# A two-layer decoder kernel: the second head's sums of weights are made in the second unit in place of the fourth

## The chip, the core and the metric

The kernel runs on one core of one Trainium2 chip. The metric is the device time of one execution, in microseconds. The core has a matrix engine (TensorE, PE in the profile; its weight loads are shown apart as PEld), a vector engine (DVE), a scalar engine (ACT), a general engine (GpSimd, POOL) and a sync engine (SP), which here issues nearly all DMAs. Each engine takes its instructions in an order fixed when the kernel is built, and waits where an instruction's inputs or buffers aren't ready.

## What is computed

The input is a sequence of 2048 rows of 1024 numbers. A retention layer comes first, then a layer of attention within a sliding window. The change touches the first layer only:

```python
proj = rmsnorm(x, g_norm) @ w_in                # 1024 -> q 1024, k 1024, v 2048, gate 2048
q, k = theta_shift(q), theta_shift(k)           # 4 heads of 256
v                                               # 4 heads of 512
o = rms(retention(q, k, v))                     # chunks of 128 rows, a state of 256 x 512 per head
x = x + (o * silu(gate)) @ w_out
```

The second layer computes one shared K and V, 16 query heads over 128 keys back with a bias and a sink, a gate and an output product. All is float32; the kernel splits operands into a high and a low part, so that one product becomes three matmuls.

## The kernel before, in words

The first layer is done in 16 **units**: four groups of 512 rows, and in each the four heads. Unit u is group u // 4, head u % 4, and units are counted from 0, so the second unit is unit 1 and the fourth is unit 3. For each unit `main` (L500) makes the products with the weights: q and k in `project_qk` (L564), then the values and the gate; `ret` (L655) does the retention of the unit in four chunks of 128 rows; `out_a` (L779) multiplies with the output weights and adds to the rows. The loop at the end of `phase_a` runs `main` of unit u + 1 together with `ret` of unit u (through `drive`, L43, which takes turns between the two) and then `out_a` of unit u.

Values and gate are made in two ways. Units 0 to 3 (`plain_vg`, L615) multiply as usual. From unit 4 on, `strassen` (L445) makes a value block and a gate block with seven products in place of eight. It needs sums and differences of weights, and of rows:

- `stage_sums(h)` (L376) makes the **sums of weights** of head h, once, and writes them to DRAM. It takes eight pieces; each piece is two loads of 256 KB (L393), four DVE operations of 128x256 (L397 to L400) and, one step later, two stores of 256 KB (L387). Head h's sums are first read in unit 4 + h.
- `row_stats(g)` (L300) loads the rows of group g (L307) and takes the mean of their squares on ACT (L309).
- `stage_rows(g)` (L317), the **row staging**, turns the result with PE (`spread`, L170), scales the rows of group g (L343), makes their sums (L347 to L350) and writes both to DRAM (L331). `load_sums` (L371) and `load_rows` (L366) read them back through `load_part` (L362, with an ACT cast at L363 and a DVE subtraction at L364). For group 1 this is called in unit 3.

These three are generators. They stand in a list, `behind`, and `step()` (L290) advances the first of the list by one; it is taken off when it has ended. `step()` is called at fixed places of the code: four times in `project_qk`, four times each in the value and the gate product of units 0 to 3, fourteen times in `strassen`, and six times in `out_a`. So units 1, 2 and 3 have 18 steps each and the units from 4 on 24. `stage_sums` takes 11 steps, `row_stats` 5 and `stage_rows` 12. Before, `behind` gets head 0 at unit 1, the row statistics and row staging of group 1 at unit 2, head 1 at unit 3, head 2 at unit 4 and head 3 at unit 5.

The places of the steps set the order of the code, which isn't the order of execution by itself: when the kernel is built, a scheduler runs through the code with a model of the times and puts an instruction on its engine as soon as its inputs are there and a buffer is free, code that comes first having the preference. Buffers come from pools by tag. All of the work in `behind`, and the split rows that `out_a` makes at the end of a group (L786), use the tag "st" with six buffers. Weights and rows that come from DRAM go through the tag "raw" with three (L118 to L126, L307, L362).

The other lines that are spoken of are in `ret`: the square of an output block (ACT, L748), the mean and power on POOL (L114, L115), the gated block (DVE, L751), its transpose (PE, L754), the state (DVE, L739 and L741), its high and low part (ACT L828, DVE L829), the products with it (PE, L726 to L728) and with the chunk (L718 to L720, L729 to L731); and in `out_a` the evacuation that adds a PSUM bank to the rows (DVE, L794). PSUM banks "a" and "b" (two each) serve all products with weights in turn, so a product can start only when the evacuations of the one before are done.

Of the kernel before, what the change touches and what calls it, by code (L numbers as in the profile page):

```python
# [42 lines left out]
def drive(tc, main, side, ratio, ahead, head=0):  # L43

    main_on = side_on = True
    due = head - ratio
    while main_on or side_on:
        due += ratio
        while main_on and (due >= 1 or not side_on):
            main_on = next(main, "end") != "end"  # L50
            due -= 1
        if side_on:
            with tc.high_priority(offset=ahead):
                side_on = next(side, "end") != "end"
# [3 lines left out]
def tile_yoco(ctx, tc, x, x_t, w_qk, w_vg, wo_a, w_kv, w_b, wo_b, ag, kvg, bg, kng, qng,  # L58
# [116 lines left out]
    def scales(g, tiles, tag, rb):  # L175

        acc, rt = tiles
        nc.sync.dma_start(acc, sqs[g])
        yield
        ps = bank(f"ssq_{g}", tag)  # L180
        for m in range(MT):
            nc.tensor.matmul(ps[:, m : m + 1], acc[:, m * P : (m + 1) * P], ones[:, :1], start=True, stop=True)
        r, eps = (small.tile([P, MT], F32, tag=f"{n}bx", bufs=2, name=f"{n}bx_{g}") for n in ("r", "e"))
        nc.vector.tensor_scalar(eps, ps[:, :MT], 1.0 / D, EPS, op0=ALU.mult, op1=ALU.add)
        nc.gpsimd.tensor_tensor(r, eps, neghalf[:, :MT], op=ALU.pow)
        nc.vector.tensor_scalar_mul(eps, eps, EPS)
        scaled[g] = r, eps, rb
        yield
        load = spread(r, rt, f"b{g}", tag)
        yield  # L190
        yield
        load(rb)
        yield
# [84 lines left out]
    def phase_a(pa):  # L278
# [9 lines left out]
        behind = []  # L288

        def step():  # L290
            if behind and next(behind[0], "end") == "end":
                behind.pop(0)
# [4 lines left out]
        def short(name):  # L297
            return p1.tile([P, 512], F32, tag="r", bufs=4, name=name)

        def row_stats(g):  # L300

            ss = small.tile([P, MT], F32, tag="ssx", bufs=2, name=f"ssx_{g}")
            r = small.tile([P, MT], F32, tag="rx", bufs=2, name=f"rx_{g}")
            st["stats", g] = ss, r
            for m in range(MT):
                xin = wp.tile([P, D], F32, tag="raw", bufs=RAW, name=f"xin_{g}_{m}")
                nc.sync.dma_start(xin, x[(g * MT + m) * P : (g * MT + m + 1) * P, :])  # L307
                junk = p1.tile([P, D], BF16, tag="st", bufs=6, name=f"jx_{g}_{m}")
                nc.scalar.activation(junk, xin, AF.Square, accum_out=ss[:, m : m + 1])  # L309
                if m == MT - 1:  # L310
                    nc.gpsimd.tensor_scalar(ss, ss, 1.0 / D, EPS, op0=ALU.mult, op1=ALU.add)
                    nc.gpsimd.tensor_tensor(r, ss, neghalf[:, :MT], op=ALU.pow)
                yield
# [62 lines left out]
        def stage_sums(h):  # L376

            vg = w_vg[h]

            d = [dram.tile([2, 2, P, 2, 512], F32, name=f"T{i}v_{h}") for i in range(2)]  # L380
            st["sums", h] = {"T2": d[0][0], "T1": d[0][1], "T4": d[1][0], "T3": d[1][1]}
            pieces = [(c, slice(256 * e, 256 * e + 256)) for c in range(4) for e in range(2)]
            raw, done = [], []
            for n in range(len(pieces) + 2):

                for c, e, i, t in done:
                    nc.sync.dma_start(d[i][:, c // 2, :, c % 2, e].rearrange("j p t -> p j t"), t)  # L387
                done = []
                if n < len(pieces):
                    c, e = pieces[n]  # L390
                    raw.append([p1.tile([P, 2, 256], F32, tag="st", bufs=6, name=f"b{h}_{n}_{i}") for i in range(2)])
                    for i in range(2):
                        nc.sync.dma_start(raw[n][i], vg[i, :, c // 2, :, c % 2, e].rearrange("j p t -> p j t"))  # L393
                if 0 < n <= len(pieces):
                    c, e = pieces[n - 1]
                    (b11, b12), (b21, b22) = [[t[:, j, :] for j in range(2)] for t in raw[n - 1]]
                    nc.vector.tensor_tensor(b22, b22, b12, op=ALU.subtract)  # L397
                    nc.vector.tensor_tensor(b12, b12, b11, op=ALU.subtract)
                    nc.vector.tensor_tensor(b11, b22, b11, op=ALU.add)
                    nc.vector.tensor_tensor(b21, b21, b11, op=ALU.subtract)  # L400
                    done = [(c, e, i, raw[n - 1][i]) for i in range(2)]
                yield

        def stage_b(pieces):

            raw, done = [], []
            for n in range(len(pieces) + 2):
                if n < len(pieces):
                    t = p1.tile(list(pieces[n][0].shape), F32R, tag="st", bufs=6, name=f"wlo_{n}")
                    nc.sync.dma_start(t.bitcast(F32), pieces[n][0])  # L410
                    raw.append(t)
                for d, i, v in done:
                    nc.sync.dma_start(d[:, i], v.bitcast(F32))
                done = []
                if 0 < n <= len(pieces):
                    t = raw[n - 1]
                    _, d, sc = pieces[n - 1]
                    hi = p1.tile(list(t.shape), F32R, tag="st", bufs=6, name=f"whi_{n}")
                    for k in range(t.shape[1]):
                        v, h = t[:, k, :], hi[:, k, :]  # L420
                        if sc is None:
                            nc.scalar.copy(h, v.bitcast(F32))
                            nc.vector.tensor_tensor(v, v.bitcast(F32), h.bitcast(F32), op=ALU.subtract)
                        else:
                            nc.scalar.mul(h, v.bitcast(F32), sc[:, k : k + 1])
                            nc.vector.scalar_tensor_tensor(v, v.bitcast(F32), sc[:, k : k + 1], h.bitcast(F32),
                                                           op0=ALU.mult, op1=ALU.subtract)
                    done = [(d, 0, hi), (d, 1, t)]
                yield
# [405 lines left out]
        for u in range(nu - 1):  # L835

            g, h = units[u + 1]
            if u + 1 in (1, 3, 4, 5):
                behind.append(stage_sums({1: 0, 3: 1, 4: 2, 5: 3}[u + 1]))
            if h == 2 and g + 1 < NG:  # L840
                behind.append(row_stats(g + 1))
                behind.append(stage_rows(g + 1))
            if u + 1 in (8, 9, 12, 13, 14, 15):
                behind.append(stage_b(todo[:9]))
                del todo[:9]
            if u + 1 == nu - 1:
                behind.append(scales(0, [short(f"stb_{i}") for i in range(2)], "rr", small.tile([P, T], F32, tag="rb", bufs=1, name="rb_0")))
            drive(tc, main(u + 1), ret(u), 2 if u + 1 < PLAIN else 3, 0)
            for _ in itertools.islice(bias, 2 if u >= RH else 0):
                pass  # L850
            if u < nu - 2:
                for _ in out_a(u):
                    step()
# [383 lines left out]
    with ExitStack() as es:  # L1237
        mk = lambda name, bufs: es.enter_context(tc.tile_pool(name=name, bufs=bufs))
        psum["phase"] = "a"
        psum["pool"] = es.enter_context(tc.tile_pool(name="psa", bufs=1, space=bass.MemoryType.PSUM))  # L1240
        phase_a(dict(v=mk("av", 4), const=mk("ca", 1), p1=mk("a1", 1), p2=mk("a2", 2), g=mk("ag", 4), xs=mk("as", 1), x1=mk("ax", MT)))
# [97 lines left out]
```

## Time and profile before

| what | value |
|---|---|
| median of 3 runs | 2459.9 us (2458.28 to 2459.98) |
| the profiled execution | 2457.89 us |
| its span, first to last instruction | 2456.2 us |
| PE busy | 2410.0 us, 98% |
| PE weight loads busy | 1963.2 us, 80% |
| DVE busy | 1592.5 us, 65% |
| ACT busy | 1056.4 us, 43% |
| POOL busy | 281.8 us, 11% |
| moved by DMA | 501.76 MB, 204 GB/s on average |

Times in the profile are microseconds from the span's start. A group's row names the line, the engine, the operation and the tiles (out<-in). In a row of instructions in order of time, the first number is the start and the second the duration, and a bracket gives how long the engine was idle before it and what ended that. In a row of waits the numbers are the sum of the waits in us, how many there were, and the longest. A row of a window gives its ends, its length and each engine's busy time with the number of instructions in parentheses. PE's matmuls overlap, so that busy time is the union of their spans. "granted clock" is the share of full speed that TensorE was given.

### The profile page before, as it was taken

The page shows a single profiled execution, that of the slowest core. Times are in us where ns is not written, and L with a number is a line of the kernel's source. Part 1 is how long each engine was busy: PE and PEld are TensorE (multiplying, and loading weights), DVE is VectorE, ACT ScalarE, POOL GpSimd, SP SyncE. Part 2 cuts the span into 40 slices and gives each one's busy share as a digit, 9 for nine tenths or more (in the row PEclk, how much of TensorE's full clock was granted, in tenths as well). Part 3 has the DMA queues.
Part 4 walks back from the last instruction along what each step waited for, and adds up shares of the span by engine and source line. Part 5 has one row for each costly group of instructions (what it writes and reads, how often), then busy time and mean ns, then how long its engine had stood idle before and what let it go on. Part 6 is the DMA issues. An engine that isn't in the chain of part 4 may idle for free.

```text
span 2456.2 us, 32234 instructions
## 1 busy us (share of the span) xinstructions
PE 2410.0 (98%) x11569; PEld 1963.2 (80%) x11569; DVE 1592.5 (65%) x2874; ACT 1056.4 (43%) x2028; POOL 281.8 (11%) x348
## 2 busy tenths in 40 slices
PE   8999999999999999999999999999999999999997
PEld 6888778888878888888888788887787787778776
DVE  5646684787768668587777864744656556466555
ACT  4333233544446356355445643533424334334332
POOL 0000000021000020000002000122202212202020
PEclk9999999999999999999999999999999999999999
DMA  8433884488676368386548953646564674665662
GB/s 286 152 112 116 280 285 129 155 300 279 210 263 216 129 238 283 129 289 224 173 155 296 342 185 103 206 147 227 202 206 146 223 258 137 206 202 185 201 230 69
DMA packets 195379, 501.76 MB, mean 204 GB/s; under 512 B 20487, under 2 KB 65748, under 8 KB 195220
## 3 DMA queue, kind: packets, MB, share of 16 engines
q1 hardware_dynamic: 195140, 499.45, 60.6%
q8 instruction: 91, 1.49, 0.2%
q14 instruction: 68, 0.56, 0.1%
q0 software_dynamic: 80, 0.26, 0.0%
HBM read 397.88 MB, written 104.90 MB: 205 GB/s over the span
## 4 chain that ended last, share of the span: by engine, by line
PE 83%; DMA 9%; DVE 4%; ACT 2%; issue 1%; SPq 1%; POOL 0%; ACTq 0%; DVEq 0%; POOLq 0%
PE pp_ao L146 4%; PE pp_ao L148 4%; PE pp_ao L147 4%; PE o_t L1153 3%; PE s_t L1104 2%; PE pp_bo L267 2%; PE pp_bo L268 2%; PE pp_bo L266 2%; PE pT_t L1135 1%; DMA xS<-xss 1%; DMA b<-in_w_vg 1%; PE dl_r L718 1%; PE dl_r L720 1%; PE ot_r L754 1%; PE dl_r L719 1%
## 5 line engine op out<-in xcount | busy, mean ns | idle before, releaser
L1107 DVE CUSTOM_DVE_ANT_0 P_t<-s_t,bias,nsnk 128x256 f32<-128x256 f32 (+1 forms) x256 | 116.5, 472 | 132.2 <-PE s_t L1104 124.4
L146 PE MATMUL pp_ao<-ohi_r,whi_ao 128*128 128x512 f32 x512 | 199.6, 391 | 0.9 <-DVE x_r L794 0.9
L147 PE MATMUL pp_ao<-olo_r,whi_ao 128*128 128x512 f32 x512 | 199.6, 390 | 0.0
L148 PE MATMUL pp_ao<-ohi_r,wlo_ao 128*128 128x512 f32 x512 | 193.7, 390 | 0.0
L1117 ACT ACTIVATE P_t<-P_t,nm_t 128x128 f32<-128x128 f32 x256 | 100.5, 395 | 113.9 <-DVE P_t L1114 111.5
L114 POOL TENSOR_SCALAR r_o_r<-sso_r,ep 128x1 f32<-128x1 f32 x48 | 36.8, 766 | 908.1 <-ACT jo_r L748 908.1
L794 DVE TENSOR_TENSOR x_r<-x_r,pp_ao 128x512 f32<-128x512 f32 x128 | 86.3, 683 | 62.1 <-PE pp_ao L148 62.0
L828 ACT CAST Shi_r<-S 128x512 fp32r<-128x512 f32 x120 | 69.8, 618 | 121.2 <-PE o_r L728 80.7
L146 PEld LDWEIGHTS pp_ao<-ohi_r,whi_ao 128*128 128x128 f32 x512 | 96.1, 188 | 21.8 <-ACT whi_a3qk L125 1.1
L148 PEld LDWEIGHTS pp_ao<-ohi_r,wlo_ao 128*128 128x128 f32 x512 | 96.1, 188 | 20.3 <-DVE wlo_ao L126 0.2
L147 PEld LDWEIGHTS pp_ao<-olo_r,whi_ao 128*128 128x128 f32 x512 | 96.1, 188 | 19.8
L1104 PEld LDWEIGHTS s_t<-kst,qst_b 128*128 128x128 f32 x512 | 83.1, 193 | 31.5 <-DVE nm_t L1107 7.5
L125 ACT CAST whi_ao<-raw_ao 128x1024 fp32r<-128x1024 f32 x64 | 67.1, 1050 | 91.2 <-DMA raw_ao<-in_wo_a 33.7
L829 DVE TENSOR_TENSOR Slo_r<-S,Shi_r 128x512 fp32r<-128x512 f32 x120 | 79.0, 686 | 37.0 <-ACT Shi_r L828 36.7
L1104 PE MATMUL s_t<-kst,qst_b 128*128 128x256 f32 (+1 forms) x512 | 98.3, 295 | 4.6 <-DVE nm_t L1107 4.6
L126 DVE TENSOR_TENSOR wlo_ao<-raw_ao,whi_ao 128x1024 fp32r<-128x1024 f32 x64 | 78.2, 1223 | 36.9 <-ACT whi_ao L125 36.7
L1141 POOL TENSOR_SCALAR_AFFINE_SELECT pTs_t<-pTs_t 128x512 f32<-128x512 f32 x60 | 40.4, 674 | 524.5 <-ACT pTs_t L1138 524.5
L741 DVE SCALAR_TENSOR_TENSOR S<-S,dl_r 128x512 f32<-128x512 f32 x112 | 74.2, 682 | 33.8 <-PE dl_r L720 33.8
L1138 ACT COPY pTs_t<-pT_t 128x512 f32<-128x512 f32 x64 | 37.4, 584 | 132.3 <-PE pT_t L1135 132.0
L267 PE MATMUL pp_bo<-olo_t,whi_bo 128*128 128x512 f32 x224 | 88.1, 393 | 0.4 <-DVE olo_t L1174 0.3
L268 PE MATMUL pp_bo<-ohi_t,wlo_bo 128*128 128x512 f32 x224 | 87.9, 393 | 0.0
L266 PE MATMUL pp_bo<-ohi_t,whi_bo 128*128 128x512 f32 x224 | 85.6, 397 | 1.2 <-ACT ohi_t L1172 1.1
(1036 smaller groups left out, 7137.8 us busy)
## 6 DMA issues: line engine op xcount, KB each, us to landing
raw_ao<-in_wo_a SPq DMA_DIRECT2D x64, 512.0 KB, 3.7
b<-in_w_vg SPq DMA_DIRECT2D x64, 256.0 KB, 5.2
res<-xmid SPq DMA_DIRECT2D x28, 512.0 KB, 6.0
whi_bo<-wo SPq DMA_DIRECT2D x28, 512.0 KB, 3.9
wlo_bo<-wo SPq DMA_DIRECT2D x28, 512.0 KB, 4.7
x_r<-in_x_t SPq DMA_DIRECT2D x16, 512.0 KB, 6.9
xin<-in_x SPq DMA_DIRECT2D x16, 512.0 KB, 3.4
T0v<-b SPq DMA_DIRECT2D x32, 256.0 KB, 5.3
```

The lines of the kernel that those rows point to most:

```text
L126: nc.vector.tensor_tensor(lo, raw, hi.bitcast(F32), op=ALU.subtract)
L146: nc.tensor.matmul(o, hi[:, kk, sl], xh, start=st, stop=False)
L147: nc.tensor.matmul(o, hi[:, kk, sl], xl, start=False, stop=False)
L148: nc.tensor.matmul(o, lo[:, kk, sl], xh, start=False, stop=sp)
L266: nc.tensor.matmul(o, hi[:, kk, sl], xh, start=s, stop=False)
L267: nc.tensor.matmul(o, hi[:, kk, sl], xl, start=False, stop=False)
L268: nc.tensor.matmul(o, lo[:, kk, sl], xh, start=False, stop=e)
L794: nc.vector.tensor_tensor(t, t, ps, op=ALU.add)
L829: nc.vector.tensor_tensor(lo, src[:, d, :], hi.bitcast(F32), op=ALU.subtract)
L1104: nc.tensor.matmul(o, q[:, h, :], kst[:, kv * 2 + hl, kb + b0 : kb + 2, :], start=hl == 0, stop=hl == 1)
L1107: nc.vector.tensor_tensor_reduce(out=pt[:, j, :w], in0=o, in1=bias[:, kv * GQ + h, b0 * P :], scale=-1.0, scalar=nsnk[:, kv * GQ + h : kv ...
L1117: nc.scalar.activation(pt[:, i, :P], pt[:, i, :P], AF.Exp, scale=-1.0, bias=nm[:, i : i + 1], accum_out=den[:, i : i + 1])
```

## The change

The list `behind` gets heads 0 and 1 together at unit 1, and nothing of heads at unit 3. Heads 2 and 3 are put in where they were, and nothing else is changed. Head 1's eleven steps then stand behind head 0's: of the 18 steps in unit 1 head 0 takes 11 and head 1 seven, its last four come in unit 2, and the row statistics and the row staging of group 1, 17 steps, follow behind these; three of the 17 fall into unit 3.

```diff
         for u in range(nu - 1):
 
             g, h = units[u + 1]
-            if u + 1 in (1, 3, 4, 5):
-                behind.append(stage_sums({1: 0, 3: 1, 4: 2, 5: 3}[u + 1]))
+            for head in {1: (0, 1), 4: (2,), 5: (3,)}.get(u + 1, ()):
+                behind.append(stage_sums(head))
             if h == 2 and g + 1 < NG:
                 behind.append(row_stats(g + 1))
                 behind.append(stage_rows(g + 1))
```

## The prediction

> **What bounds the kernel now.** I read the page's head and its chain first, then PE's busy time unit by unit, then PE's waits in the unit that stands out, then the streams of single engines there. Units are counted from 0: the second unit is unit 1, the fourth is unit 3.
>
> ```profile
> span 2456.2 us, 32234 instructions
> PE 2410.0 (98%) x11569; PEld 1963.2 (80%) x11569; DVE 1592.5 (65%) x2874; ACT 1056.4 (43%) x2028; POOL 281.8 (11%) x348
> PE 83%; DMA 9%; DVE 4%; ACT 2%; issue 1%; SPq 1%; POOL 0%; ACTq 0%; DVEq 0%; POOLq 0%
> ```
>
> PE is busy for 2410.0 of 2456.2 us. A change that leaves the matmuls alone can only win from the 46.2 us in which PE waits, or from stretches at a lower clock; it can lose by making a new wait. The next rows are units 0 to 5 (length, then busy time of PE, PEld, DVE, ACT, POOL, PE's granted clock, DMA share, GB/s).
>
> ```profile
> 7.40:80.80 73.40, 70.21 (x306) 57.25 (x306) 44.14 (x69) 28.29 (x36) 5.67 (x10) 1.00 0.89 295
> 80.80:186.40 105.60, 105.60 (x489) 87.56 (x487) 54.64 (x71) 37.50 (x54) 5.97 (x11) 1.00 0.31 103
> 186.40:290.80 104.40, 103.36 (x474) 85.29 (x474) 65.27 (x103) 34.26 (x49) 5.56 (x11) 1.00 0.56 182
> 290.80:406.00 115.20, 109.20 (x488) 89.08 (x489) 83.26 (x132) 42.07 (x58) 5.47 (x8) 0.99 0.75 242
> 505.30:604.00 98.70, 98.70 (x457) 81.15 (x456) 80.07 (x122) 47.43 (x73) 14.72 (x15) 1.00 0.82 285
> ```
>
> Units 1 to 3 have the same products. Units 1 and 2 take 105.6 and 104.4 us, unit 3 takes 115.2, of which PE is idle for 6.0. Unit 3 is 10.2 us over the mean of the two others (105.0): no gain in it can well be larger. Unit 1 has the lightest DMA (0.31) and DVE (54.64 us). What ended PE's waits between 290 and 331 us:
>
> ```profile
> PE ot_r L754 <- DVE gate_a L751: 2.5, 1, 2.5
> PE pp_a3qk L596 <- DVE x_r L794: 2.2, 1, 2.2
> PE o_r L727 <- DVE Slo_r L829: 0.8, 1, 0.8
> PE kt_r L697 <- DVE olo_r L760: 0.3, 1, 0.3
> ```
>
> Together 5.8 of the 6.0 us, all by a late DVE and all before 331. The first one is followed by a slow stretch (a window row again; PE's clock is the 0.51):
>
> ```profile
> 326.10:329.40 3.30, 3.29 (x10) 2.81 (x11) 1.97 (x5) 0.00 (x0) 0.00 (x0) 0.51 0.68 204
> ```
>
> In 3.3 us at 0.51 about 1.6 us are lost (3.3 x 0.49). Unit 3's accountable loss is 6.0 + 1.6 = 7.6 us. [...]
>
> **The change part by part.** First, where the sums of weights really run. The loads of their pieces (L393) in four windows, and the first products of the row staging (L343) and the transpose that starts it (L170):
>
> ```profile
> L393 SPq DMA_DIRECT2D b<-in_w_vg x16: 368/373/963, 36.9 to 72.1; - x16
> L393 SPq DMA_DIRECT2D b<-in_w_vg x16: 368/398/877, 270.1 to 306.3; - x16
> L393 SPq DMA_DIRECT2D b<-in_w_vg x16: 368/373/570, 311.0 to 356.3; - x16
> L393 SPq DMA_DIRECT2D b<-in_w_vg x16: 367/378/672, 513.2 to 565.2; - x16
> L170 PE MATMUL rt_x<-ident_r,rx x1: 271/271/271, 239.3 to 239.3; 128*4 128x128 f32 x1
> L343 DVE SCALAR_TENSOR_TENSOR xst<-xst,ags,rbx x8: 741/752/753, 245.2 to 268.9; 128x512 f32<-128x512 f32 x8
> ```
>
> Each head has 16 loads. Head 0's run in unit 0, before their steps are due in unit 1; head 1's begin right behind the last product of the row staging (268.9, then 270.1), at the end of unit 2; head 2's begin at 311.0, right behind head 1's, a whole unit before their steps in unit 4 (from 406). So the six "st" buffers, handed out in the order of the code, decide when this work runs, and it runs as early as they let it. Behind head 2, "st" goes to the rows of unit 3's output products, which aren't there before its end. From this I work out what moves.
>
> *Head 1 goes into unit 1.* Behind head 0 it starts at about 73; the four sets of loads took 35.2, 36.2, 45.3 and 52.0 us, so it ends at 109 to 125. That adds to units 0 and 1 sixteen loads and sixteen stores on SP's queue (32 x 256 KB, 8.4 MB) and 32 DVE operations at 0.42 us (rows below), 13.4 us; DVE would be busy for 68 of unit 1's 105.6 us. The 8.4 MB in 36 us are 233 GB/s on top of unit 1's 103, about 336, more than any unit row shows (295), so loads will be slow and DVE, which takes its instructions in order, will wait for them. What such waits may cost is seen where DVE's results are next used:
>
> ```profile
> 92.14 0.75 DVE L751 SCALAR_TENSOR_TENSOR gate_a<-o_r,r_o_r,gate_a 128x512 f32<-128x512 f32 x1
> 92.80 0.68 DVE L829 TENSOR_TENSOR Slo_r<-S,Shi_r 128x512 fp32r<-128x512 f32 x1
> 97.35 0.60 PE L754 MATMUL ot_r<-ident_r,gate_a 128*128 128x128 f32 x4
> 100.08 0.39 PE L727 MATMUL o_r<-Slo_r,qhi_r 128*128 128x512 f32 x1
> 60.22 0.43 DVE L397 TENSOR_TENSOR b<-b,b 128x256 f32<-128x256 f32 x1 [4.58 <-issue]
> PE pp_a0g L150 <- DVE vlo_a L524: 2.3, 1, 2.3
> ```
>
> The gated block is ready at 92.9 and used at 97.35, the state's low half is ready at 93.5 and used at 100.08: 4.5 and 6.6 us of room. In unit 0 head 0's operation held DVE for 4.58 us and PE then waited 2.3. In unit 5 head 3's loads ran beside 98.70 us in which PE was never idle. So the bounds are 0 and 2.3 us; with room of 4.5 I take 0.8. SP's queue gets these transfers ahead of unit 1's weights; the matmuls that use the weights are the waiting party, and the same bounds hold for that.
>
> *Head 1 leaves the end of unit 2 and the start of unit 3, but head 2 moves up.* Four steps of head 1 are left over for unit 2 (22 steps against 18 there), so the row statistics and the row staging stand four steps later. The transpose at 239.3 was due in the second quarter of the value product and is then due in the second quarter of the gate product:
>
> ```profile
> L150 PE MATMUL pp_a2v<-whi_a2v,xhi_a x32: 389/389/397, 217.4 to 242.9; 128*128 128x512 f32 x32
> L150 PE MATMUL pp_a2g<-whi_a2g,xhi_a x32: 389/389/476, 244.4 to 265.6; 128*128 128x512 f32 x32
> ```
>
> The gate product's quarters are about 5.3 us, so 250 instead of 239.3: everything behind it on "st" comes some 11 us later. Row staging then ends at about 280, head 2's loads begin at 281 and end at 317 to 326. The stretch from 281 to 326 stays as full as it is, with one head's work where there were parts of two; only 326 to 356 empties, and there PE lost nothing but the 1.6 us. So I can't book the 7.6 us as gone. The stalls, one by one:
>
> ```profile
> 295.04 0.42 DVE L397 TENSOR_TENSOR b<-b,b 128x256 f32<-128x256 f32 x1 [2.91 <-issue]
> 295.39 0.68 DVE L794 TENSOR_TENSOR x_r<-x_r,pp_ao 128x512 f32<-128x512 f32 x1
> 318.39 0.62 ACT L828 CAST Shi_r<-S 128x512 fp32r<-128x512 f32 x1 [4.22 <-DVE S L741]
> 321.34 1.05 ACT L363 CAST xhi_S<-xb_S 128x1024 fp32r<-128x1024 f32 x1 [2.33 <-DMA xb_S<-xS]
> 322.82 0.59 ACT L748 ACTIVATE jo_r<-o_r 128x512 bf16<-128x512 f32 x1
> L397 DVE TENSOR_TENSOR b<-b,b 128x256 f32<-128x256 f32 x12 | 5.1, 421 | 7.8 <-issue 4.4 <-DMA b<-in_w_vg 3.3
> ```
>
> The 2.2 us: a piece's first operation held DVE for 2.91 us ahead of the evacuation that frees PE's bank. Head 2's first pieces will stand at the same place. The 2.5 us and the slow clock: ACT waited 2.33 us for the row sums' load, so the squares at 322.82, and with them the gated block, were late. That load stays, in less traffic. Each may stay or go; I keep half: 3.8 of 7.6 stay, 3.8 are won.
>
> *The row staging, later by 11 us,* now meets the evacuations of unit 2's output product at about 278. PE's only wait in unit 2 is there:
>
> ```profile
> 279.52 0.47 PE L146 MATMUL pp_ao<-ohi_r,whi_ao 128*128 128x512 f32 x1 [0.93 <-DVE x_r L794]
> ```
>
> It can go (-0.9) or grow to the 2.2 us that the same kind of wait cost at 295 (+1.3); I take +0.5.
>
> The sum is -3.8 + 0.8 + 0.5 = -2.5 us. The profiled execution took 2457.89 us, 1.7 over its span, and 2.0 below the median of 2459.9. So 2455.4 by that execution and 2457.4 against the median. A measurement of this kernel tells about 0.2% from no change, 4.9 us, and the forecast lies within that. From unit 4 on the code's order is unchanged, and I count nothing there. This case's own ends: all that it adds comes at its top (2.3 + 1.3) with the stalls half gone, -0.2, and all at its bottom (0 - 0.9), -4.7: 2455.2 to 2459.7.
>
> **The rivals.**
>
> *Unit 3 is cleared (faster).* If head 2's pieces fall behind the evacuations at 290 to 297 and the row sums' loads land in time, all 7.6 us go: -7.6 + 0.8 + 0.5 = -6.3, 2453.6; with the unit's whole excess of 10.2, 2451.0. For it: head 3 cost PE nothing where it ran alone (unit 5). Against it: the stretch isn't emptied.
>
> *Nothing moves (same).* Head 2 takes head 1's place to the letter and unit 1 hides its part: 0 us, 2459.9. For it: room of 4.5 us in unit 1, and the same ingredients at 290 to 326. Against it: half the pieces, later by 11 us, will hardly meet the same waits.
>
> *The row sums come too late (slower).* Their loads must follow the last store of the row staging, and ACT's cast of them stands ahead of the squares of the retention.
>
> ```profile
> 296.27 0.41 SPq L362 DMA_DIRECT2D xb_S<-xS  x1
> 301.48 1.05 ACT L363 CAST xhi_S<-xb_S 128x1024 fp32r<-128x1024 f32 x1 [9.00 <-DMA xb_S<-xS]
> 270.50 2.05 SPq L331 DMA_DIRECT2D xS<-xss  x4
> ```
>
> The last stores are issued by 272.6, the load at 296.27: 23.7 us of room, from which the store's landing goes off. A shift of 11 us fits, one of over some 20 doesn't; the three steps that are now in unit 3 could bring that if they weren't run ahead. Beyond that point the cast, already 9.00 us in waiting, would hold the squares until about 8 us later, and PE with them: 6 us of wait and another 1.6 at half clock, so -2.5 + 7.6 = +5.1, 2465.0.
>
> **How the numbers follow.** The forecast 0.54, cleared 0.24, nothing moves 0.13, too late 0.09. Below 2455.0 (faster by over 0.2%) lie most of cleared, 0.22, and 0.04 of the forecast whose losses go further than half: 0.26. Above 2464.8 lie most of too late: 0.07. The rest, 0.67, is within 0.2%. The range takes in the forecast's ends, nothing moves with the runs' own spread, and cleared nearly to its far end, and leaves out too late: 2451.5 to 2462.0.
>
> **What would show it.** Right: loads of the second head at 73 to 125; the row staging's transpose near 250; head 2's loads from about 281 to 326, and nothing of the kind behind that until unit 5; unit 1 still about 105.6 to 107 us long, unit 3 near 111, with one or two of PE's four waits left. Wrong: head 2's loads that stay at 311, since then "st" isn't what orders them; a wait of PE on the gated block in unit 1; unit 3 at 105 (cleared) or with ACT's cast waiting past 305 (too late); a difference that lies behind unit 4.

## The result and the profile after

| what | before | changed |
|---|---|---|
| median of 22 runs | 2460.03 us | 2465.66 us |
| ratio, with its 95% interval | | 1.0021 (1.0014 to 1.0027) |
| the profiled execution | 2457.89 us | 2462.84 us |
| its span | 2456.2 us | 2461.1 us |

The change makes the kernel slower by 0.2%, some 5 us. The prediction was 2457.4 us, within 2451.5 to 2462.0: a gain of 2.5 us was forecast, and the measured median lies above the whole range. The 22 runs of before include one of 4568.4 us, which the ratio leaves out.

First the units 0 to 3 of the changed kernel, from its windows: ends, length, busy time of PE, PEld, DVE, ACT and POOL, PE's granted clock, DMA share, GB/s. The third and fourth row are units 2 and 3.

```profile
7.30:79.60 72.30, 70.74 (x306) 57.87 (x306) 44.80 (x72) 28.26 (x36) 5.65 (x10) 1.00 0.91 305
79.60:188.00 108.40, 105.40 (x484) 86.24 (x482) 63.26 (x99) 33.80 (x49) 6.52 (x11) 1.00 0.50 162
188.00:302.90 114.90, 107.71 (x486) 88.93 (x485) 70.65 (x110) 38.84 (x56) 5.71 (x11) 0.97 0.59 190
302.90:408.30 105.40, 105.03 (x483) 86.83 (x483) 68.50 (x95) 40.66 (x55) 4.70 (x8) 1.00 0.52 173
```

Unit 3 went from 115.2 to 105.4 us, and unit 2 from 104.4 to 114.9: the long unit is one earlier. Unit 1 went from 105.6 to 108.4. Unit 0 ends 1.2 us sooner. By the start of unit 4 (406.0 before, 408.3 now) 2.3 us of the profile's 4.9 are lost; the other 2.6 come behind it, 1.3 of them in unit 7 and 0.9 in unit 9 (101.7 before, 102.6 now). PE's waits in units 1, 2 and 3, from three answers:

```profile
PE pp_a1v L150 <- DVE th_a L608: 1.5, 1, 1.5
PE ot_r L754 <- DVE gate_a L751: 1.0, 2, 0.8
PE dl_r L720 <- DVE klo_r L702: 0.5, 1, 0.5
PE pp_ao L146 <- DVE x_r L794: 7.2, 1, 7.2
PE ot_r L754 <- DVE gate_a L751: 0.4, 1, 0.4
```

The first three are new and lie in unit 1. The fourth is unit 2's: one wait of 7.2 us for the evacuation in the middle of the output product. Of unit 3's waits 0.4 us are left. The clock fell after the long wait (the 0.52):

```profile
288.70:293.40 4.70, 4.69 (x11) 3.70 (x12) 4.70 (x9) 0.00 (x0) 0.00 (x0) 0.52 0.99 301
```

That is another 2.3 us (4.7 x 0.48). Where the work was put, from the rows of the loads, the transpose and the staging's products, and of the first load of row sums:

```profile
L393 SPq DMA_DIRECT2D b<-in_w_vg x32: 367/382/1252, 36.3 to 109.1; - x32
L393 SPq DMA_DIRECT2D b<-in_w_vg x16: 368/440/1064, 279.4 to 316.1; - x16
L170 PE MATMUL rt_x<-ident_r,rx x1: 271/271/271, 246.3 to 246.3; 128*4 128x128 f32 x1
L343 DVE SCALAR_TENSOR_TENSOR xst<-xst,ags,rbx x8: 747/752/753, 252.0 to 278.2; 128x512 f32<-128x512 f32 x8
302.92 0.42 SPq L362 DMA_DIRECT2D xb_S<-xS  x1
```

Heads 0 and 1 load up to 109.1 us. The staging is 7 to 9 us later, and head 2 follows it at 279.4. DVE in order of time, around the long wait:

```profile
278.21 0.75 DVE L343 SCALAR_TENSOR_TENSOR xst<-xst,ags,rbx 128x512 f32<-128x512 f32 x1 [3.59 <-DMA xst<-in_x_t]
282.08 0.69 DVE L684 TENSOR_TENSOR slo_r<-s_r,shi_r 128x512 fp32r<-128x512 f32 x1
286.16 0.43 DVE L397 TENSOR_TENSOR b<-b,b 128x256 f32<-128x256 f32 x1 [3.39 <-DMA b<-in_w_vg]
287.54 0.42 DVE L400 TENSOR_TENSOR b<-b,b 128x256 f32<-128x256 f32 x1
287.88 0.68 DVE L794 TENSOR_TENSOR x_r<-x_r,pp_ao 128x512 f32<-128x512 f32 x1
```

And the same place in the kernel before:

```profile
276.97 0.43 DVE L397 TENSOR_TENSOR b<-b,b 128x256 f32<-128x256 f32 x1 [4.64 <-DMA b<-in_w_vg]
278.69 0.68 DVE L794 TENSOR_TENSOR x_r<-x_r,pp_ao 128x512 f32<-128x512 f32 x1
```

The brackets are to be read together with what stands next. The evacuation (L794) stands at the same place of DVE's order in both: its start is 1.7 us behind that of the first piece's first operation. Before, that piece also held DVE, for 4.64 us, but early enough that PE waited only 0.9. Now the staging's tail held DVE for 3.59, the first piece for 3.39, and the evacuation behind both came 9.2 us later than before (287.88 against 278.69).

### The profile page after: what moved, and what is told of

Read it like the earlier page. It is cut to its first block, busy times and chain, and to the rows that moved or that the text cites. A ratio compares the mean times of both kernels' runs of the same rounds, so it can differ in the third digit from the quotient of the medians.

```text
span 2461.1 us, 32236 instructions
## 1 busy us (share of the span) xinstructions
PE 2412.4 (98%) x11569; PEld 1965.5 (80%) x11569; DVE 1591.8 (65%) x2874; ACT 1054.8 (43%) x2028; POOL 279.6 (11%) x348
## 4 chain that ended last, share of the span: by engine, by line
PE 84%; DMA 8%; DVE 4%; ACT 2%; issue 1%; SPq 1%; POOL 0%; DVEq 0%; ACTq 0%; POOLq 0%
PE pp_ao L146 4%; PE pp_ao L148 4%; PE pp_ao L147 4%; PE o_t L1153 3%; PE s_t L1104 2%; PE pp_bo L267 2%; PE pp_bo L268 2%; PE pp_bo L266 2%; DMA b<-in_w_vg 1%; PE pT_t L1135 1%; PE ot_r L754 1%; PE dl_r L718 1%; PE dl_r L720 1%; PE dl_r L719 1%; PE o_r L726 1%; PE o_r L728 1%
## 5 line engine op out<-in xcount | busy, mean ns | idle before, releaser
L1117 ACT ACTIVATE P_t<-P_t,nm_t 128x128 f32<-128x128 f32 x256 | 100.5, 394 | 113.2 <-DVE P_t L1114 110.9
L794 DVE TENSOR_TENSOR x_r<-x_r,pp_ao 128x512 f32<-128x512 f32 x128 | 85.9, 684 | 59.2 <-PE pp_ao L148 59.0
```

The costliest lines, as they stand in the source:

```text
L794: nc.vector.tensor_tensor(t, t, ps, op=ALU.add)
L1117: nc.scalar.activation(pt[:, i, :P], pt[:, i, :P], AF.Exp, scale=-1.0, bias=nm[:, i : i + 1], accum_out=den[:, i : i + 1])
```

## The experiments

Each of the eleven runs below the changed kernel was timed in five rounds against the kernel before, whose median in those rounds was 2460.5 to 2461.2 us; their ratios go by that. Lengths of units run from the first matmul of a unit's q and k product to that of the next, in the run's profiled execution.

| run | unit 1 | unit 2 | unit 3 | median us | ratio to before, 95% interval |
|---|---|---|---|---|---|
| before | 105.6 | 104.4 | 115.2 | 2460.03 | |
| changed | 108.4 | 114.9 | 105.4 | 2465.66 | 1.0021 (1.0014 to 1.0027) |
| four idle steps only | 105.7 | 113.1 | 108.5 | 2459.56 | 0.9988 (0.9975 to 1.0001) |
| heads 0 and 1 paired | 109.5 | 110.5 | 109.6 | 2466.12 | 1.0021 (1.0008 to 1.0033) |
| head 2 late | 110.3 | 107.5 | 105.0 | 2461.53 | 0.9996 (0.9983 to 1.0009) |
| three heads early | 111.0 | 102.9 | 106.2 | 2455.64 | 0.9981 (0.9970 to 0.9992) |
| head 1 without operations | 105.6 | 113.2 | 108.7 | 2461.20 | 1.0005 (0.9995 to 1.0016) |
| head 1 without loads | 105.7 | 113.3 | 106.7 | 2459.37 | 1.0000 (0.9987 to 1.0013) |
| three heads early, on POOL | 120.9 | 105.4 | 104.9 | 2461.15 | 1.0004 (0.9993 to 1.0015) |
| paired, head 2 late | 110.2 | 105.4 | 104.9 | 2455.17 | 0.9977 (0.9966 to 0.9988) |
| head 1 held back | 105.7 | 102.9 | 116.9 | 2456.40 | 0.9982 (0.9973 to 0.9990) |
| changed, head 2 held back | 108.7 | 108.5 | 106.4 | 2459.75 | 0.9999 (0.9989 to 1.0010) |
| head 1 held back, head 2 late | 105.6 | 103.0 | 108.9 | 2454.93 | 0.9980 (0.9969 to 0.9990) |

The first four tell two theories apart. Theory A: the loss is the place of the row staging and of the pieces behind it, in unit 2. Theory B: the loss is what the second head costs beside unit 1.

**Four idle steps only** is the kernel before with the delay and without the move:

```diff
             if h == 2 and g + 1 < NG:
+                if u + 1 == 2:
+                    behind.append(iter(range(3)))
                 behind.append(row_stats(g + 1))
```

> The kernel before, with four idle steps put ahead of the row statistics and the row staging of group 1; the heads stay where they were, so head 1 isn't made in unit 1. Theory A (the place: the row staging's tail and the first pieces of the head behind it come later and hold DVE in front of the evacuations in the middle of unit 2's output product): PE waits 5 to 9 us for the evacuation in unit 2, as in the changed kernel, and the ratio to the kernel before is 1.0015 to 1.0035. Theory B (the load: the second head's transfers and operations beside unit 1 cost the time): units 1 and 2 stay at 105.6 and about 104.4 us, the ratio is within 0.9990 to 1.0010.

```profile
PE pp_ao L146 <- DVE x_r L794: 7.2, 1, 7.2
185.70:298.80 113.10, 105.85 (x475) 87.14 (x473) 65.91 (x104) 36.50 (x53) 5.58 (x11) 0.95 0.58 184
298.80:407.30 108.50, 106.86 (x488) 87.88 (x488) 82.90 (x132) 42.28 (x58) 4.83 (x8) 1.00 0.77 251
```

The delay alone makes unit 2's 7.2 us wait, as A said, with head 1's pieces at the place where head 2's stand in the changed kernel. But unit 3 gets 6.7 us shorter in return, and the time is no longer than before. So A has the wait right and the loss wrong: the four steps move a loss of about one size from unit 3 to unit 2. B has the time about right (0.9988, where 0.9990 to 1.0010 was said) and unit 2 wrong, which was to stay at 104.4.

**Heads 0 and 1 paired** undoes the delay and keeps the move:

```diff
+        def paired(gen):
+            while next(gen, "end") != "end" and next(gen, "end") != "end":
+                yield
...
-                behind.append(stage_sums(head))
+                behind.append(paired(stage_sums(head)) if u == 0 else stage_sums(head))
```

> The changed kernel, with heads 0 and 1 advanced two parts at a step, so that both end within unit 1's steps and the row statistics and row staging stand at the steps they had before the change. Theory A: the transpose of the row staging is back near 239 us, head 2's loads start near 270, PE's wait in unit 2 is at most 1.5 us, the losses at the start of unit 3 come back in part, and what is left over is what units 0 and 1 pay for head 1 (about 1.6 us): ratio 0.9990 to 1.0015. Theory B: unit 1 stays at 108 us or more and the ratio stays at 1.0014 to 1.0027, with the row staging's place of no account.

The ratio stayed at 1.0021, as B said, though its interval (1.0008 to 1.0033) reaches into A's window up to 1.0015. A's details failed: the transpose came at 242.1, the loads began at 276.9 and not near 270, and PE still waited 4.4 us in unit 2. Unit 2 now starts 2 us later, and the staging ended later in it, though its steps were those of before; why wasn't followed further.

**Head 2 late** takes head 2 away from the end of unit 2; **three heads early** does that and undoes the delay too:

```diff
-            for head in {1: (0, 1), 4: (2,), 5: (3,)}.get(u + 1, ()):
+            for head in {1: (0, 1), 5: (2, 3)}.get(u + 1, ()):        # head 2 late
...
+            for head in {1: (0, 1, 2), 5: (3,)}.get(u + 1, ()):       # three heads early, with paired() at u == 0
```

(The comments in this diff and in the next ones are added here.)

> The changed kernel, with head 2 put in at unit 5 ahead of head 3, behind the split rows of unit 3's output product, so that it can't run before them. Theory A: no pieces of a head stand in front of unit 2's evacuations; PE's wait there falls from 7.2 us to what the row staging's tail makes alone, 0 to 3.5 us; unit 3 stays near 105 us; two heads beside units 5 and 6 cost 0 to 3 us: ratio 0.9975 to 1.0005. Theory B: units 0 and 1 are as in the changed kernel and so is the ratio, 1.0014 to 1.0027.

> Heads 0, 1 and 2 all in unit 1, two parts at a step (18 steps, all of unit 1's), head 3 at unit 5 as it was. The row staging stands where it was before the change and no head runs between it and unit 5. Theory A: unit 2's wait at most 1 us, unit 3 near 105 us, units 0 and 1 pay 1.6 to 3.5 us: 7 to 8 us less and 2 to 3.5 more, ratio 0.9965 to 0.9992. Theory B: half as much again beside unit 1, which costs more than in the changed kernel: ratio 1.0020 to 1.0045.

With head 2 late PE still waits 1.9 us in unit 2, unit 3 is 105.0, and units 5 and 6 pay 3.9 us together, more than the 3 that was said; the ratio, 0.9996, is in A's window and not in B's. With three heads early the rows of units 1 to 3 are these:

```profile
79.90:190.90 111.00, 106.98 (x490) 87.33 (x489) 76.16 (x134) 37.48 (x54) 7.22 (x11) 1.00 0.76 247
190.90:293.80 102.90, 102.90 (x476) 85.38 (x474) 62.25 (x90) 34.03 (x49) 5.55 (x11) 1.00 0.49 159
293.80:400.00 106.20, 106.20 (x490) 88.14 (x489) 64.93 (x81) 42.63 (x58) 5.29 (x8) 1.00 0.41 130
```

With no pieces between the staging and unit 5, PE has no wait at all in units 2 and 3 (busy time equals length), even with three heads beside unit 1, which then takes 111.0. So nearly all of the loss in units 2 and 3 is the pieces' there (the late staging alone, in the run with head 2 late, makes 1.9 us). The loss in unit 1 is real too: unit 2 starts at 190.9 here, 4.5 us later than before, where 1.6 to 3.5 was said. Neither theory alone gives the time.

The next two ask what in unit 1 costs. The changed kernel's DVE shows a suspect:

```profile
87.20 0.43 DVE L397 TENSOR_TENSOR b<-b,b 128x256 f32<-128x256 f32 x1 [5.02 <-DMA b<-in_w_vg]
DVE b L397 <- DMA b<-in_w_vg: 10.7, 6, 5.0
```

In unit 1 pieces held DVE for 10.7 us in six waits, before the change for none.

```diff
-                    nc.vector.tensor_tensor(b22, b22, b12, op=ALU.subtract)
...
+                    if h != 1:                                       # head 1 without operations: the four lines
+                        nc.vector.tensor_tensor(b22, b22, b12, op=ALU.subtract)
...
-                    for i in range(2):
+                    for i in range(2 if h != 1 else 0):              # head 1 without loads; its operations read cos
```

> The changed kernel, with head 1's four operations of each piece left out, so that its pieces are loaded and stored unchanged (the sums of head 1 are then not made). All its transfers stay. Theory B1 (in unit 1 DVE, which works in order, waits for the loads of head 1's pieces): unit 1 goes back to 105.5 to 106.5 us without waits of PE; unit 2 keeps its wait of 4 to 8 us on the evacuation, since head 2 stands where it did; ratio 1.0003 to 1.0018. Theory B2 (the traffic itself delays unit 1's weights): unit 1 stays at 108 us or more, ratio as for the changed kernel, 1.0014 to 1.0027.

> The changed kernel, with head 1's sixteen loads left out and its 32 operations working on a table that lies in SBUF already; the stores stay (the sums of head 1 are then not made). Theory B1 (the wait for the loads): unit 1 at 105.5 to 106.5 us although DVE does as much work as in the changed kernel; ratio 1.0003 to 1.0018. Theory C (32 more operations crowd DVE): unit 1 stays at 107.5 us or more and the ratio at 1.0014 to 1.0027. With B2, half of head 1's traffic is left and half of the loss, about 107 us.

Unit 1 of the two runs, without operations and without loads:

```profile
79.00:184.60 105.60, 105.60 (x488) 87.57 (x487) 54.63 (x71) 35.40 (x50) 5.97 (x11) 1.00 0.51 167
```
```profile
79.00:184.70 105.70, 105.70 (x490) 87.63 (x489) 63.06 (x96) 35.37 (x50) 8.26 (x11) 1.00 0.40 130
```

Both runs leave out part of head 1's work, so its sums aren't made. The first has all of the changed kernel's traffic (0.51, 167 GB/s) and no loss; the second has its DVE work (63.06 us against 63.26) and no loss. In neither does DVE wait for a piece in unit 1. It takes both: an operation in DVE's order that waits for a load. B1 is shown, B2 and C fall. Both runs keep unit 2's wait, 8.0 us, and are still within the noise of the kernel before, as the run with idle steps is.

**Three heads early, on POOL** puts the operations of the pieces elsewhere:

```diff
-                    nc.vector.tensor_tensor(b22, b22, b12, op=ALU.subtract)
+                    nc.gpsimd.tensor_tensor(b22, b22, b12, op=ALU.subtract)
```

> Heads 0, 1 and 2 in unit 1 as in the run with three early heads, but the four operations of each piece on POOL instead of DVE. Theory B1: DVE no longer waits for pieces, so unit 1 falls from 110.9 us to 105.5 to 108, the wait of PE in unit 0 on the values' low part goes too, ratio 0.9955 to 0.9980. Rival: POOL works in order as well, so the mean and power of each output block (two small operations on POOL) wait behind the pieces, the gated block is late, and unit 1 stays at 110 us or more: ratio 0.9985 to 1.0030.

```profile
PE ot_r L754 <- DVE gate_a L751: 11.7, 4, 5.5
POOL b L397 <- DMA b<-in_w_vg: 11.3, 7, 3.7
```

The rival was right, and by more than it said: the wait moved to POOL (11.3 us), the gated blocks came late, and unit 1 took 120.9 us. The operations are longer there, too: in unit 1 the means of the four lines are 0.80 to 0.95 us, against 0.42 on DVE, and POOL was busy for 63.6 us. How much of the loss is the wait and how much the longer operations wasn't separated. Units 2 and 3, without pieces, were clean again.

**Paired, head 2 late** joins two of the edits above.

> Heads 0 and 1 in unit 1, two parts at a step; heads 2 and 3 both at unit 5. So no head stands between the row staging and unit 5, and the row staging is at the steps it had before the change. If the wait in unit 2 comes from the first pieces behind the row staging: unit 2 at 103 to 106 us, unit 3 at 105 to 106, unit 1 at 109 to 110.5, and units 5 and 6 pay 1 to 4 us for head 2: ratio 0.9975 to 1.0000. If it comes from something else that the two heads in unit 1 bring: unit 2 stays at 110 us or more, ratio 1.0005 to 1.0025.

It is the fastest by the middle of its interval, 0.9977, though three others (0.9980 to 0.9982) can't be told from it: unit 1 still pays (110.2), units 2 and 3 are clean (105.4, 104.9, without a wait).

The last three hold a head back, by small copies that take all six "st" buffers and need unit 3's finished q:

```diff
+        def hold():
+            for i in range(6):
+                nc.gpsimd.tensor_copy(stp(f"hold_{i}")[:, :1], st["qk"][:, 1, :1])
+            yield
...
+            if u + 1 == 3:                      # on the kernel before: in front of head 1
+                behind.extend([iter(range(3)), hold()])
...
+            if u + 1 == 3:                      # on the changed kernel: in front of head 2
+                behind.extend([iter(range(1)), hold()])
...
+            for head in {1: (0,), 3: (1,), 5: (2, 3)}.get(u + 1, ()):   # third run, with the first hold
```

> The kernel before, with head 1 where it was at unit 3, but held back: six small copies out of unit 3's finished q take the six st buffers ahead of head 1's first piece, so that no piece can be loaded before about 336 us. Theory (pieces cost PE time only where DVE waits for their loads ahead of work that PE needs soon, and the end of unit 2 and the start of unit 3 are such places): unit 1 at 105.7 us, unit 2 at 102.5 to 105, unit 3 at 105 to 107.5 us with at most 1.5 us of waits; 8 to 11 us less than before, ratio 0.9955 to 0.9975. Rival (the pieces cost the same few us wherever they run beside a unit with the plain products): the wait shows up later in unit 3 or at the start of unit 4, which then takes over 101 us: ratio 0.9985 to 1.0010.

> The changed kernel, with head 2 held back in the same way until unit 3's q is done. Theory: unit 0 and 1 as in the changed kernel (unit 1 at 108 to 109 us), unit 2 without the 7.2 us wait, at 104 to 108 us with what the late row staging makes alone, unit 3 at 105 to 106.5 us: ratio 0.9970 to 1.0000, above the run with head 1 held back by what unit 1 pays. Rival: the row staging, not head 2's pieces, makes the wait in unit 2, which stays at 110 us or more: ratio 1.0010 to 1.0030.

> Head 0 at unit 1, head 1 held back in unit 3 by the six small copies, heads 2 and 3 both at unit 5: one head only runs in unit 3 and none in units 1 and 2. Theory: unit 1 at 105.7, unit 2 at 102.5 to 104.5, units 3 and 4 together at 205 to 210 us (before: 214.5) if the gate's weights come in time with one head less in their way, units 5 and 6 pay 0 to 3 us: ratio 0.9955 to 0.9978. Rival: the wait for the gate's weights of unit 3 stays (3.6 us and the half clock behind it, as with heads 1 and 2 there): units 3 and 4 together at 211 us or more, ratio 0.9978 to 0.9990.

Unit 3's wait with heads 1 and 2 held back to it, and unit 2's wait in the changed kernel with head 2 held back:

```profile
PE pp_a3g L150 <- ACT whi_a3g L125: 3.6, 1, 3.6
```
```profile
PE pp_ao L146 <- ACT khi_r L702: 2.9, 1, 2.9
```

With head 1 held back unit 2 was clean, but PE waited 3.6 us in unit 3 for the weights of the gate: the gain was half of the one expected. Here it was the order on SP's queue and not DVE's: the last load of those weights went out at 362.58, right behind a load of a piece at 362.11 that SP had held for 2.7 us until a store had landed. (Unit 4 is 95.0 us there and the two units together 211.9, against 214.5, since part of the retention falls on the other side of the boundary: unit 3 has 511 matmul records against 488.) The third run has 1.3 of the 3.6 us left and units 3 and 4 at 208.4, in the theory's window; its ratio, 0.9980, lies just outside that window and in the rival's. The changed kernel with head 2 held back loses the 7.2 us wait, keeps 2.9 us in unit 2, keeps unit 1's loss, and stands at 0.9999: holding back that one head takes away what the change had cost. The 2.9 us are put down to an ACT operation that ended at 283.91. The evacuation, right behind the staging's tail, ended at 283.87, and so would have held PE about as long by itself. By that the late staging alone costs some 2.9 of the 7.2 us, and head 2's pieces the other 4.3.

## Why the prediction was wrong

**Where the work runs: right in the main.** "st" orders it. Loads of heads 0 and 1 to 109.1 (109 to 125 was said), the transpose at 246.3 (250), head 2's loads from 279.4 to 316.1 (281 to 326), none behind that until unit 5. The 11 us for four steps were too many, and that 246.3 is so near 250 is partly luck: counted from unit 2's start, the transpose comes after 52.9 us before the change, 57.0 with the four idle steps alone and 58.3 in the changed kernel, whose unit 2 also starts 1.6 us later.

**Unit 3: too little.** Half of 7.6 us was to stay; unit 3 got 9.8 us shorter, with 0.4 us of waits left. "Head 2's first pieces will stand at the same place" is what failed: they stood some 16 us ahead of unit 3's start, at the evacuations in the middle of unit 2's output product. The rival "unit 3 is cleared" had this unit right.

**Unit 2: the step that failed.** "It can go (-0.9) or grow to the 2.2 us that the same kind of wait cost at 295 (+1.3); I take +0.5." Measured: 7.2 us and 2.3 at half clock where there were 0.9, so +8.6 of unit 2's +10.5; another 1.1 us are retention products that PE now does before unit 3's first product (301.81 to 302.94) and did behind it before. The term counted the row staging's tail alone, and its top came from a wait of PE, the nearest of its kind. What it left out is head 2's pieces, which follow the staging and stand in front of the same evacuation: with head 2 held back 2.9 us of the 7.2 are left. A bound could have come from the trace of before: there a piece held DVE for 4.64 us up to 276.97, and the evacuation started 1.7 us behind it, at 278.69. If the two keep their order, what makes the piece late makes the evacuation late; they kept it, and both came 9.2 us later. The same ingredients, later, were reckoned with for unit 3 alone.

**Unit 1: too small.** +0.8 within 0 to 2.3 was said; unit 1 took 2.8 more, unit 0 1.2 less, together +1.6, inside the bounds and twice the value taken. The room of 4.5 us was measured at one place of the chain, and the longest hold was 5.02 at the start of it. That DVE's waits for loads would be the cause was right, as the two runs with half of head 1 show; the fear for the weights was not.

**Behind unit 4: counted at nothing.** The profile has 2.6 us there, 1.3 of it in unit 7 (below) and 0.9 in unit 9. Seven of the profiles have the same work behind the start of unit 4: the kernel before, the changed one, four idle steps, paired, head 1 without operations, head 1 without loads, and the changed one with head 2 held back. They take from 2050.2 to 2057.5 us for it, and the kernel before is the shortest, so 2.6 us can't be told from the spread between single executions.

**The rivals.** "Too late" gave 2465.0, close to the median, by a mechanism that didn't happen: the row sums' first load went out at 302.92, and no wait of PE hangs on it. Its point of decision, a shift of over 20 us, wasn't reached. The time of a rival that comes true is no proof of it. Three of the prediction's own signs of being wrong came: a wait of PE on the gated block in unit 1 (1.0 us), unit 3 at 105.4, and a difference behind unit 4.

The sum, with the measured terms of the profiled execution: -9.8 (unit 3) + 10.5 (unit 2) + 1.6 (units 0 and 1) + 2.6 (behind) = +4.9, where -3.8 + 0.5 + 0.8 + 0 was written. By the runs, units 2 and 3 exchange a loss of about the same size, which the idle steps alone do without a cost that can be measured, and what is added is unit 1's. Taking either unit 1's wait or unit 2's collision away brings the time back to that of before. What stays open is the size: units 0 to 3 account for 2.3 us in the profile, and the medians differ by 5.6. Where the rest lies, the single profiles don't tell.

One reading of the prediction's rows, on which no term hangs: its five rows are units 0 to 3 and 5, and the last one ends at 604.0, while unit 5 lasts to 611.5 (106.2 us, PE without a wait up to there).

## What to carry to other kernels

Work that fills DVE's idle time carried its waits for loads with it: in unit 1 pieces held DVE for 10.7 us and the unit took 108.4, where head 1's loads without its operations left it at 105.6 and its operations without its loads at 105.7. The price wasn't the busy time of DVE (63.26 and 63.06 us) but what stood behind a piece when its load was late. When such work is shifted, take each hold that the trace shows, move it by the shift, and see on which evacuation or chain it lands. It is worth more to keep it away from the end of a product than to find it an emptier unit: the fastest runs here (0.9977 to 0.9982) have nothing waiting for loads between the row staging and the start of unit 3's products. That alone isn't enough: head 2 late has nothing there either, but a later staging, and stayed at 0.9996, and with three heads on POOL unit 1 lost what units 2 and 3 won (1.0004).

## What was not expected of the hardware

In these traces the length of a wait doesn't fix the clock after it. At the start of unit 7 PE waits about as long in both kernels. The granted clock in the window behind it is 0.64 in the changed kernel, whose rows come first, and 1.00 in the one before:

```profile
711.92 0.47 PE L596 MATMUL pp_a7qk<-xhi_a,whi_a7qk 128*128 128x512 f32 x1 [2.45 <-DVE x_r L794]
711.90:716.00 4.10, 4.08 (x12) 3.24 (x13) 4.10 (x6) 2.24 (x4) 0.79 (x1) 0.64 1.01 295
```
```profile
709.47 0.47 PE L596 MATMUL pp_a7qk<-xhi_a,whi_a7qk 128*128 128x512 f32 x1 [2.35 <-DVE x_r L794]
709.50:714.00 4.50, 4.50 (x20) 3.71 (x21) 4.50 (x6) 2.25 (x4) 1.17 (x1) 1.00 1.03 344
```

That is 1.5 us (4.1 x 0.36), about as much as the whole of unit 7's difference, behind waits of 2.45 and 2.35 us. In unit 3 of the kernel before, a wait of 2.46 us was followed by 0.51 (326.1 to 329.4). In the changed kernel with head 2 held back an even longer wait, of 2.92 us, was followed by a clock of 1.00 (284.0 to 288.7, and 1.00 for unit 2 as a whole). So a wait of 2.35 to 2.92 us may be followed by a slow stretch in one execution and not in another, and a single profile can't tell a change of 1 to 2 us from that. What sets the clock, these traces don't show.
